# A two-layer decoder step on one core: weights split further ahead, products ordered by kind, memory caches loaded earlier, norm sums on GpSimd

## The chip, the cores and the metric

One core of a Trainium2 chip. The metric is the device time of one execution in microseconds (us). The engines are TensorE (PE in the profile), VectorE (DVE), ScalarE (ACT), GpSimd (POOL) and the queue of SyncE (SP), which only issues transfers here. ACT and POOL issue transfers too.

## What is computed

The reference is one inference step of a decoder with two layers over 576 tokens (512 of a prompt, 64 of eight samples), width 1024, all in float32. Each layer has three branches on the same input, which are merged by sigmoid gates and projected; then a squared-ReLU MLP. Cut to what matters:

```
rq, rk, rv, rg, sq, sk, sv, mq, g_r, g_s, g_m = split(x @ w_in)
mk, mv  = mem_prompt @ w_mem_kv              # the prompt's memory; the samples' is cached
ret_b   = (silu(rg) * group_norm(retention(rq, rk, rv))) @ w_br_ret
swa_b   = sliding_window_attention(sq, sk, sv) @ w_br_swa
mem_b   = softmax(mq @ km.T) @ vm @ w_br_mem # km, vm: mk, mv or cache_mem_k, cache_mem_v
merged  = sigmoid(g_r)*ret_b + sigmoid(g_s)*swa_b + sigmoid(g_m)*mem_b
x = layer_norm(ALPHA*x + merged @ w_out)
h = square(relu(x @ w_up))
x = layer_norm(ALPHA*x + h @ w_down)
```

## The kernel before

**Products.** A float32 product is made of three products of rounded parts: with w = hi + lo and x = xh + xl, it sums hi·xh, lo·xh and hi·xl. The tokens stand in two groups, A and B, of 288 columns. A unit is 128 output rows of one weight (a tile of 128x1024, 512 KB): 8 slots of 128 input channels, 3 matmuls each, 24 matmuls for one group. `gemm` writes the three matmuls of a slot after each other.

**Splitting.** A unit of weights is loaded by SP into a T tile (there are 38 of them) and split before use: its hi part is a CAST on ACT or DVE, its lo part a TENSOR_TENSOR on DVE. If its use is more than FAR = 11 us ahead, the lo part is instead a negated copy on ACT and a transfer from POOL that adds the raw weights to it (the T<-T transfers). The order of all instructions is decided while the program is built: `tick` goes through the units in order of use and splits the next one either when ScalarE is expected to be free, or, whatever ScalarE has to do, when its use is less than LEAD = 4 us ahead. A unit that is not split by then is split right ahead of its matmuls (`run`). A cap limits the tiles in flight; it differs by stage.

**Stages of a layer.** Memory keys and values mk, mv; four rounds of retention projections (rk, rq, rv, rg); sliding-window projections; gates and branch outputs (gr, br, gs, bs, gm, bm), between whose matmuls the attention work of the three branches is interleaved by generators; the output projection wo (8 units for A, then 8 for B) with the first norm; the up projection (8 units for A, then 8 for B, and so on); the pairs, which multiply sums and differences of blocks; the down projection dn with the second norm. Then the next layer starts with mk, mv.

**Memory attention of the samples** (`mem_sample`, once for each group and layer) takes four batch entries. Each needs a 512 KB tile of cached keys (in_mck) and later one of cached values (in_mcv), loaded by POOL. Two key tiles are asked for well ahead (`mem_ahead`), the other two after the matmuls of the first and the second:

```
yield Pe((kt[b], qz))
for h in range(4): T.matmul(ps[...], lhsT=qz[:, b, h, :], rhs=kt[b][:, h, :], ...)
if b < 2: kt.append(self.mem_load("mck", l, f * 4 + b + 2))
```

and the value tiles likewise: two after the last key matmul, the others after the first and second value product.

**Norm** (`norm_ev`). Each output unit of wo and dn is added to the residual tile on DVE (T<-T,pg), then to a running sum (accA, accB), and from unit 4 on its square (ACT) to a sum of squares (tiles s, rc). `half` shifts and squares units 0 to 3. After unit 7, `last` takes both sums through PE, forms the reciprocal root on ACT (Ln, Exp) and DVE, subtracts the mean and multiplies on DVE, and makes the xh parts (ACT, 128x288 with par) and xl parts (DVE, 128x576) of the next stage's input. All sums are on DVE.

Every instruction is recorded by one helper, so that the profile shows line L359 nearly everywhere; tiles tell the stages apart. The functions that the change touches follow.

Of the kernel before, what the change touches and what calls it, by code (L numbers as in the profile page):

```python
# [24 lines left out]
EPS = 1e-5  # L25
# [12 lines left out]
EARLY_PE = -0.8  # L38
LEAD = 4.0
FAR = 11.0  # L40
# [409 lines left out]
class Builder:  # L450
# [72 lines left out]
    def soonest(self, choices, *ins):  # L523
# [3 lines left out]
        return getattr(self.nc, min(choices, key=lambda x: max(c.te[x[0]], t) + x[1])[0])  # L527

    def rounded(self, hi, src):
        n = src.free_size()  # L530
        e = self.soonest((("scalar", 0.094 + n / 1200.0), ("vector", 0.2 + n / 1920.0)), src)
        (e.copy if e is self.nc.scalar else e.tensor_copy)(hi, src)
# [14 lines left out]
    def split(self, i):  # L547
        u, k, b = self.items[i]
        if b is not None:
            self.w[i] = self.block(u, b)  # L550
            self.live[i] = 1
            return
        raw = self.raw.pop(u)
        hi = self.tile([P, 8, P], F32R)
        lo = self.tile([P, 8, P], F32R)
        if self.use[i] - self.fill.t > FAR and k[1] not in ("mq", "gs", "bs", "gm", "bm") and u > 15:
            self.nc.scalar.copy(hi, raw)
            self.nc.scalar.activation(lo, raw, AF.Copy, scale=-1.0)
# [65 lines left out]

    def gemm(self, ps, u, slots, xs, first=True):
        hi, lo = self.w[u]
        mm = self.nc.tensor.matmul
        n = len(slots)
        cols = ps.shape[1]
        for i, s in enumerate(slots):  # L630
            xh, xl = xs(i)
            mm(ps, lhsT=hi[:, s, :], rhs=xh, start=(first and i == 0), stop=False, skip_group_check=not first)
            mm(ps, lhsT=lo[:, s, :], rhs=xh, start=False, stop=False, skip_group_check=not first)
            mm(ps, lhsT=hi[:, s, :], rhs=xl, start=False, stop=(i == n - 1), skip_group_check=not first)
            if i % 2 and i < n - 1:
                self.fill.advance(6 * mm_us(cols))

    def mstep(self, u, g, X, evac, slots=range(8), tag="g"):
        n = NG[g]

        def fn():
            ps = self.bank(tag)[:, :n]
            self.gemm(ps, u, list(slots), lambda i: (X[g]["h"][i // 4][:, i % 4, :], X[g]["l"][i // 4][:, i % 4, :]))
            evac(g, ps)
        return ([u], fn, 6 * mm_us(n))

    def both(self, u, X, evac, slots=range(8), tags="gg"):
        return [self.mstep(u, g, X, evac, slots, tag) for g, tag in zip("AB", tags)]

# [180 lines left out]

    def norm_ev(self, g, y, l, gi, eps, out, scale=None):

# [23 lines left out]
        def shift():  # L856
            pm = self.bank("a")[:, :n]
            yield from mean(pm, st["acc"])
            yield (pm,)
            st["c"] = self.u(n)  # L860
            V.tensor_scalar(st["c"], pm, 4.0, None, ALU.mult)
            cb = st["c"].unsqueeze(1).to_broadcast([P, 4, n])
            self.nc.vector.tensor_tensor(y[1], y[1], cb, ALU.subtract)

        def half():
            c = st.pop("c")
            V.tensor_tensor(y[0], y[0], c.unsqueeze(1).to_broadcast([P, 4, n]), ALU.subtract)
            sq = self.tile([P, 4, n])
            S.activation(sq, y[0], AF.Square)
            yield (sq,)  # L870
            V.scalar_tensor_tensor(st["acc"], c, -4.0, st["acc"], ALU.mult, ALU.add)
            self.nc.vector.tensor_tensor(sq[:, 0:2], sq[:, 0:2], sq[:, 2:4], ALU.add)
            self.nc.vector.tensor_tensor(sq[:, 0], sq[:, 0], sq[:, 1], ALU.add)
            self.nc.vector.tensor_tensor(st["s2"], st["s2"], sq[:, 0], ALU.add)

        def last():
# [17 lines left out]
            if out is None:  # L894
                V.tensor_tensor(y[1], y[1], mb, ALU.subtract)
            V.tensor_tensor(y[0], y[0], mb, ALU.subtract)
# [22 lines left out]
            def end(i):  # L919
# [3 lines left out]
                h = out[g]["h"][j][:, k]  # L923
                self.nc.vector.tensor_tensor(out[g]["l"][j][:, k], y[j][:, k], h.bitcast(F32), ALU.subtract)
            if out is not None:
# [28 lines left out]
        def ev(m, ps):  # L954
# [7 lines left out]
            if m == 0:  # L962
# [4 lines left out]
                return  # L967
            self.nc.vector.tensor_tensor(st["acc"], st["acc"], yt, ALU.add)
            if m == 1:
# [7 lines left out]
            elif m > 4:  # L977
# [4 lines left out]
                if m == 7:  # L982
                    self.fill.flush()
                    self.nc.vector.tensor_tensor(st["s2"], st["s2"], sq, ALU.add)
                    st["last"] = last()
                    self.fill.add(st["last"], 0)
                else:
                    self.fill.later(lambda: self.nc.vector.tensor_tensor(st["s2"], st["s2"], sq, ALU.add),
                                    2.0, sq)
# [420 lines left out]
    def mem_sample(self, kt, l, f, mq, ME):  # L1410
# [20 lines left out]
        m = self.small(1, "zm")  # L1431
# [39 lines left out]
    def layer(self, l, X):  # L1471
# [78 lines left out]
        for p in range(4):  # L1550
# [14 lines left out]
            steps += self.both(uid["rk", p], X, rope_ev(1)) + self.both(uid["rq", p], X, rope_ev(0))  # L1565
            if p == 0 and l:
# [238 lines left out]
        for m, g in [(m, g) for g in "AB" for m in range(SKEW_UP)] \  # L1805
                + [(m, g) for m in range(SKEW_UP, 8) for g in "AB"]:
            steps.append(self.lazy(self.mstep(uid["up", m], g, X1, up_ev(m, H[m // 4])), lambda g=g: n1[g].st["last"]))
        self.run(steps, SKEW_UP)
# [55 lines left out]
        if True:  # L1864
            keys = [("dn", m) for m in range(8)]
            n2 = {g: self.norm_ev(g, y[g], l, 16, EPS, X2) for g in "AB"}
            if X2 is not None:
# [90 lines left out]
```

## Time and profile before

| | |
|---|---|
| median of 3 runs | 2208.03 us (2206.8 to 2208.1) |
| profiled execution | 2205.09 us |
| its span (first to last instruction) | 2203.2 us |
| PE busy | 2131.3 us, 97% |
| DVE busy | 1285.2 us, 58% |
| ACT busy | 929.2 us, 42% |
| POOL busy | 151.0 us, 7% |
| mean granted clock of TensorE | 0.983 |

The profile covers one execution. Busy time of PE includes matmuls at a reduced clock: the profile gives the clock that was granted as a share of full speed (1.00 is 2.4 GHz, 0.50 is 1.2 GHz). Times in rows are counted from the start of the span.

### The profile page before, as it was taken

To read this page: it belongs to the slowest core of one execution; us is meant where nothing else is said; L and a number is where in the kernel's file an instruction comes from. 1 tells how busy PE (TensorE), PEld (TensorE's weight loads), DVE (VectorE), ACT (ScalarE), POOL (GpSimd) and SP (SyncE) were. 2 spreads that over 40 slices of the span, in tenths; PEclk is the share of its full clock that TensorE was granted. 3 is DMA by queue.
4 is the path that set the end of the run, shared out by engine and by line. 5 is a ranking of instruction groups with operands and counts; after the bars stand their busy time and mean duration, and the time that the engine had idled before them with its cause. 6 is when DMAs were issued, how large, how long until landed. Compare 5 with 4: busy or idle time off the path is not lost.

```text
span 2203.2 us, 39044 instructions
## 1 busy us (share of the span) xinstructions
PE 2131.3 (97%) x16180; PEld 2066.1 (94%) x16180; DVE 1285.2 (58%) x2752; ACT 929.2 (42%) x1757; POOL 151.0 (7%) x213
## 2 busy tenths in 40 slices
PE   9999999999998999999899999999999989999997
PEld 8999999988998999999889999999899989999997
DVE  6555644454558466666755556444545585666667
ACT  4343355223146445445444333552231465444452
POOL 0111101000000000000011111010000000000000
PEclk9999999999999999999999999999999999999999
DMA  8455745333363422224565556453342634222231
GB/s 310 112 150 138 175 116 122 118 115 133 108 187 87 108 93 96 77 89 153 142 195 141 147 143 173 107 133 106 118 142 96 189 85 116 103 77 87 96 102 57
DMA packets 83297, 277.73 MB, mean 126 GB/s; under 512 B 9072, under 2 KB 18800, under 8 KB 83056
## 3 DMA queue, kind: packets, MB, share of 16 engines
q1 hardware_dynamic: 50944, 168.27, 21.9%
q0 software_dynamic: 27088, 99.10, 19.9%
q10 hardware_dynamic: 5088, 7.87, 1.1%
q8 instruction: 127, 2.08, 0.4%
q14 instruction: 50, 0.41, 0.1%
HBM read 200.89 MB, written 15.99 MB: 98 GB/s over the span
## 4 chain that ended last, share of the span: by engine, by line
PE 85%; issue 6%; DVE 5%; DMA 2%; ACT 1%; SPq 0%; POOL 0%; DVEq 0%; POOLq 0%; ACTq 0%
PE pg L359 63%; PE pa L359 22%; DVE T L359 4%; DMA T<-in_wall 1%; ACT T L359 1%; DMA T<-in_mck 1%; ACT u L359 1%; DMA T<-in_mcv 0%; DMA T<-T 0%; DVE u L359 0%; DVE ln L359 0%; SPq L359 0%; DVE accB L359 0%; DVE rc L359 0%; DVE s L359 0%
## 5 line engine op out<-in xcount | busy, mean ns | idle before, releaser
L359 PE MATMUL pg<-T,T 128*128 128x288 f32 (+1 forms) x11840 | 1648.9, 297 | 33.0 <-DVE T L359 21.6
L359 PEld LDWEIGHTS pg<-T,T 128*128 128x128 f32 x11840 | 1599.5, 190 | 56.9 <-DVE T L359 25.6
L359 PE MATMUL pa<-T,T 128*128 128x288 f32 (+8 forms) x3368 | 456.8, 308 | 20.9 <-DMA T<-in_mck 7.9
L359 ACT CAST T<-T 128x1024 fp32r<-128x1024 f32 (+7 forms) x501 | 383.1, 797 | 185.2 <-DVE T L359 100.7
L359 PEld LDWEIGHTS pa<-T,T 128*128 128x128 f32 (+3 forms) x3368 | 400.0, 176 | 47.2 <-DMA T<-in_mck 10.7
L359 DVE TENSOR_TENSOR T<-T,T 128x1024 fp32r<-128x1024 f32 (+7 forms) x448 | 389.8, 889 | 85.7 <-ACT T L359 75.0
L359 POOL DMA_DIRECT2D T<-T x115 | 98.7, 858 | 1485.1 <-ACT T L359 1092.1
L359 ACT ACTIVATE t<-pg 128x288 f32<-128x288 f32 x128 | 52.7, 412 | 263.8 <-PE pg L359 261.1
L359 ACT ACTIVATE T<-T 128x1024 fp32r<-128x1024 f32 (+1 forms) x127 | 135.5, 1067 | 14.9 <-DVE T L359 10.8
L359 ACT ACTIVATE u<-u 128x288 f32<-128x288 f32 x200 | 88.8, 444 | 92.4 <-DVE u L359 88.4
L359 DVE TENSOR_TENSOR T<-u,T 128x288 fp32r<-128x288 f32 x160 | 72.3, 454 | 77.6 <-ACT T L359 77.6
L359 ACT COPY T<-pg 128x512 f32<-128x512 f32 (+2 forms) x44 | 21.0, 480 | 216.0 <-PE pg L359 216.0
L359 ACT CAST T<-u 128x288 fp32r<-128x288 f32 x160 | 69.3, 433 | 56.3 <-DVE u L359 52.3
L359 DVE TENSOR_TENSOR T<-T,u 128x288 f32<-128x288 f32 (+2 forms) x136 | 88.0, 660 | 3.6
L359 DVE SCALAR_TENSOR_TENSOR T<-t,pg 128x288 f32<-128x288 f32 x64 | 29.0, 453 | 94.0 <-ACT t L359 76.1
L359 DVE TENSOR_TENSOR T<-T,pg 128x288 f32<-128x288 f32 x128 | 57.5, 449 | 38.4 <-PE pg L359 38.0
L359 DVE TENSOR_TENSOR u<-u,pa 128x288 f32<-128x288 f32 x72 | 32.7, 454 | 80.2 <-PE pa L359 79.8
L359 DVE TENSOR_TENSOR T<-pa,T 128x512 fp32r<-128x512 f32 (+2 forms) x48 | 25.1, 534 | 81.0 <-ACT T L359 80.6
L359 DVE TENSOR_TENSOR T<-T,pa 128x288 f32<-128x288 f32 (+1 forms) x92 | 52.2, 568 | 17.7 <-PE pa L359 15.5
L359 DVE SCALAR_TENSOR_TENSOR u<-t,pg 128x288 f32<-128x288 f32 x64 | 28.7, 448 | 44.4 <-PE pg L359 44.4
L359 ACT CAST T<-pa 128x512 fp32r<-128x512 f32 (+2 forms) x40 | 17.3, 438 | 52.9 <-PE pa L359 48.9
L359 PE MATMUL pa<-cst,T 128*128 128x128 f32 (+1 forms) x306 | 39.6, 272 | 0.0
(157 smaller groups left out, 1041.5 us busy)
## 6 DMA issues: line engine op xcount, KB each, us to landing
T<-in_wall SPq DMA_DIRECT2D x305, 512.0 KB, 3.6
T<-T POOLq DMA_DIRECT2D x115, 512.0 KB, 5.5
T<-in_mck POOLq DMA_DIRECT2D x16, 512.0 KB, 4.4
T<-in_mcv POOLq DMA_DIRECT2D x16, 512.0 KB, 5.1
T<-in_s POOLq DMA_DIRECT2D x8, 512.0 KB, 7.6
out_state_s<-T POOLq DMA_DIRECT2D x8, 512.0 KB, 4.0
T<-in_xT SPq DMA_DIRECT2D x4, 576.0 KB, 11.0
T<-in_xT ACTq DMA_DIRECT2D x4, 576.0 KB, 6.8
```

The costliest lines, as they stand in the source:

```text
L359: r = f(*a, **kw)
```

## The change

Six edits. LEAD goes from 4 to 13. `gemm` goes through the slots three times, once for each kind of part; for late="w" the order is hi·xh, hi·xl, lo·xh, for late="x" (the first unit of the retention keys and of up) hi·xh, lo·xh, hi·xl. The two remaining key tiles are asked for right after the masked queries, ahead of the first matmul, and a value tile after each key matmul. The sums of the norms go to DVE or GpSimd, whichever the build's clock expects to be done first (`pick`); in the last norm of a group GpSimd also subtracts the mean from one half and makes one of four multiplications. Of the blocks of dh only the first may be split by way of POOL's transfers. In the down projection of layer 0 the cap is 9 instead of 7, so that the splits of the next layer's memory input may be placed there.

```diff
-LEAD = 4.0
+LEAD = 13.0
...
+    def pick(self, *ins, bias=0.0):
+        n = ins[0].free_size()
+        return self.soonest((("vector", 0.068 + n / 960.0 + bias), ("gpsimd", 0.15 + n / 480.0)), *ins)
...
-        if self.use[i] - self.fill.t > FAR and k[1] not in ("mq", "gs", "bs", "gm", "bm") and u > 15:
+        if self.use[i] - self.fill.t > FAR and k[1] not in ("mq", "gs", "bs", "gm", "bm") and u > 15 \
+                and (k[1] != "dh" or k[2] == 0):
...
-        for i, s in enumerate(slots):
-            xh, xl = xs(i)
-            mm(ps, lhsT=hi[:, s, :], rhs=xh, start=(first and i == 0), stop=False, skip_group_check=not first)
-            mm(ps, lhsT=lo[:, s, :], rhs=xh, start=False, stop=False, skip_group_check=not first)
-            mm(ps, lhsT=hi[:, s, :], rhs=xl, start=False, stop=(i == n - 1), skip_group_check=not first)
-            if i % 2 and i < n - 1:
-                self.fill.advance(6 * mm_us(cols))
+        order = ((hi, 0), (hi, 1), (lo, 0)) if late == "w" else ((hi, 0), (lo, 0), (hi, 1))
+        for k, (w, e) in enumerate(order):
+            for i, s in enumerate(slots):
+                j = k * n + i
+                self.nc.tensor.matmul(ps, lhsT=w[:, s, :], rhs=xs(i)[e], start=(first and j == 0), stop=(j == 3 * n - 1),
+                                      skip_group_check=not first)
+                if j % 6 == 5 and j < 3 * n - 1:
+                    self.fill.advance(6 * mm_us(cols))
...
             if out is None:
-                V.tensor_tensor(y[1], y[1], mb, ALU.subtract)
+                G.tensor_tensor(y[1], y[1], mb, ALU.subtract)
...
-                V.tensor_tensor(y[j][:, k], y[j][:, k], rb, ALU.mult)
+                e = G if i == 3 and out is None else V
+                e.tensor_tensor(y[j][:, k], y[j][:, k], rb, ALU.mult)
...
-            self.nc.vector.tensor_tensor(st["acc"], st["acc"], yt, ALU.add)
+            self.pick(yt, st["acc"], bias=0.0 if m in (1, 7) else bias).tensor_tensor(st["acc"], st["acc"], yt, ALU.add)
...
+        kt += [self.mem_load("mck", l, f * 4 + b) for b in (2, 3)]
+        vt = []
...
-            if b < 2:
-                kt.append(self.mem_load("mck", l, f * 4 + b + 2))
-        vt = [self.mem_load("mcv", l, f * 4 + b) for b in range(2)]
+            vt.append(self.mem_load("mcv", l, f * 4 + b))
...
-            if b < 2:
-                vt.append(self.mem_load("mcv", l, f * 4 + b + 2))
...
-                     7 if X2 else 8)
+                     9 if X2 else 8)
```

In the built program POOL issues 21 more T<-T transfers and gets 58 additions and multiplications (most of 128x288) and one ISA instruction ahead of the first of them; DVE has 79 fewer TENSOR_TENSOR and 20 more CAST, ACT 20 fewer CAST and 21 more ACTIVATE. The number of matmuls and of SP's transfers is the same. Three places follow; numbers behind an underscore are tile numbers in the order in which the program asks for them, and "-" is a row of before, "+" one of the change.

POOL, memory attention of group A in layer 0, the key and value tiles behind the two that are asked for ahead:

```order
 L359 DMA T_5010<-in_mck 128x1024
 L359 DMA T_5012<-in_mck 128x1024
-L359 DMA T_5336<-in_mck 128x1024
-L359 DMA T_5342<-in_mck 128x1024
+L359 DMA T_5270<-in_mck 128x1024
+L359 DMA T_5272<-in_mck 128x1024
+L359 DMA T_5340<-in_mcv 128x1024
+L359 DMA T_5346<-in_mcv 128x1024
 L359 DMA T_5352<-in_mcv 128x1024
-L359 DMA T_5354<-in_mcv 128x1024
-L359 DMA T_5456<-in_mcv 128x1024
-L359 DMA T_5466<-in_mcv 128x1024
```

The key tiles were the 5336th and 5342nd tile asked for and are the 5270th and 5272nd; the last two value tiles were asked for about a hundred tiles after the first two, and now stand in one run with them.

ACT, end of the branch outputs and start of the output projection in layer 0. T_6653 (before) and T_6632 (now) are the raw weights of wo's unit 1 (the second), T_6734 now those of unit 2, t and u belong to the branch outputs. Before:

```order
L359 ACTIVATE t_6732<-pg_6707 128x288
L359 CAST T_5891<-u_6747 128x288
L359 CAST T_5895<-u_6765 128x288
L359 CAST T_5891<-u_6783 128x288
L359 CAST T_5895<-u_6801 128x288
L1778 ACT_TABLE_LOAD
L359 CAST T_6822<-T_6653 128x1024
```

Now:

```order
L359 ACTIVATE t_6732<-pg_6707 128x288
L359 CAST T_6736<-T_6632 128x1024
L359 ACTIVATE T_6737<-T_6632 128x1024
L359 CAST T_5891<-u_6754 128x288
L359 CAST T_5895<-u_6772 128x288
L359 CAST T_5891<-u_6790 128x288
L359 CAST T_5895<-u_6808 128x288
L1784 ACT_TABLE_LOAD
L359 CAST T_6829<-T_6734 128x1024
```

The second unit of the output projection was cast behind the table load, and is now cast and copied ahead of four branch outputs, its lo part by way of POOL.

ACT, the norm of group B in layer 0 (ln tiles) between the evacuations of up's units for group A (pg to u to T). Before:

```order
L359 ACTIVATE ln_7588<-pa_7428 128x288
L359 ACTIVATE ln_7599<-u_7596 128x288
L359 ACTIVATE ln_7599<-ln_7599 128x288
L359 ACTIVATE u_7616<-pg_7579 128x288
L359 ACTIVATE u_7616<-u_7616 128x288
L359 CAST T_7434<-u_7616 128x288
L359 CAST T_7648<-T_7521 128x1024
```

Now:

```order
L359 ACTIVATE ln_7618<-pa_7430 128x288
L359 ACTIVATE u_7626<-pg_7597 128x288
L359 ACTIVATE u_7626<-u_7626 128x288
L359 CAST T_7436<-u_7626 128x288
L359 ACTIVATE u_7656<-pg_7631 128x288
L359 ACTIVATE u_7656<-u_7656 128x288
L359 CAST T_7436<-u_7656 128x288
L359 ACTIVATE ln_7663<-u_7660 128x288
L359 ACTIVATE ln_7663<-ln_7663 128x288
```

Ln and Exp of the norm stood right behind its square, and now stand behind the evacuations of two of group A's units; the cast of the weights that followed is no longer at this place.

## Rows read from the trace of the kernel before

**Rows 1.** The page, busy time of each engine.
```profile
PE 2131.3 (97%) x16180; PEld 2066.1 (94%) x16180; DVE 1285.2 (58%) x2752; ACT 929.2 (42%) x1757; POOL 151.0 (7%) x213
```

**Rows 2.** What PE waited for: total us, times, longest us.
```profile
PE pg L359 <- DVE T L359: 21.6, 15, 4.1
...
PE pg L359 <- ACT T L359: 11.1, 4, 7.5
...
PE pa L359 <- DMA T<-in_mck: 7.9, 4, 3.8
...
PE pa L359 <- DMA T<-in_mcv: 7.9, 4, 3.8
```

**Rows 3.** Timeline, memory attention, layer 0: start us, us, engine, work, [idle before].
```profile
481.25 1.05 POOL L359 DMA_DIRECT2D T<-in_mck  x2 [30.37 <-PE pa L359]
...
485.18 1.08 PE L359 MATMUL pa<-T,T 128*32 128x256 f32 x8 [3.82 <-DMA T<-in_mck]
...
498.02 0.53 POOL L359 DMA_DIRECT2D T<-in_mcv  x1 [0.43 <-PE pa L359]
...
501.97 1.08 PE L359 MATMUL pa<-T,T 128*32 128x128 f32 x16 [3.83 <-DMA T<-in_mcv]
```

**Rows 4.** Stretches at half clock, both layers: us, PE busy, PEclk, DMA share, GB/s.
```profile
483.30:490.13 6.83, 4.76 (x27) 0.50 0.82 314
...
500.37:507.19 6.82, 5.05 (x44) 0.50 0.43 154
...
1582.39:1589.22 6.83, 5.75 (x31) 0.50 0.83 315
...
1599.46:1606.28 6.82, 5.73 (x47) 0.50 0.38 133
```

**Rows 5.** The page, DMA issues: KB each, median us from issue to landing.
```profile
T<-T POOLq DMA_DIRECT2D x115, 512.0 KB, 5.5
...
T<-in_mck POOLq DMA_DIRECT2D x16, 512.0 KB, 4.4
```

**Rows 6.** Timeline of PE, second output-projection unit, layer 0.
```profile
631.46 0.40 PE L359 MATMUL pg<-T,T 128*128 128x288 f32 x1 [1.38 <-ACT T L359]
...
632.72 1.68 PE L359 MATMUL pg<-T,T 128*128 128x288 f32 x8 [0.86 <-DVE T L359]
```

**Rows 7.** Stretches at half clock: output projection, up projection, start of layer 1.
```profile
633.49:636.90 3.41, 3.41 (x17) 0.50 0.46 157
...
705.17:711.99 6.82, 5.00 (x21) 0.50 0.20 77
...
1090.87:1101.11 10.24, 4.01 (x17) 0.50 0.27 91
```

**Rows 8.** Timeline, up projection of layer 0, from group A to group B.
```profile
706.99 5.68 PE L359 MATMUL pg<-T,T 128*128 128x288 f32 x24 [3.77 <-DVE T L359]
...
714.76 9.50 PE L359 MATMUL pg<-T,T 128*128 128x288 f32 x58 [2.09 <-DVE T L359]
...
722.83 0.41 ACT L359 ACTIVATE u<-pg 128x288 f32<-128x288 f32 x1 [1.84 <-PE pg L359]
```

**Rows 9.** Timeline of PE, memory keys and values, start of layer 1.
```profile
1096.33 0.80 PE L359 MATMUL pg<-T,T 128*128 128x256 f32 x2 [7.48 <-ACT T L359]
...
1117.75 7.34 PE L359 MATMUL pg<-T,T 128*128 128x512 f32 x24 [3.44 <-DVE T L359]
```

**Rows 10.** Timeline of PE, start of the down projection, layer 0.
```profile
1026.47 0.40 PE L359 MATMUL pa<-T,T 128*128 128x288 f32 x1 [1.01 <-ACT T L359]
...
1036.50 5.73 PE L359 MATMUL pg<-T,T 128*128 128x288 f32 x41 [0.86 <-DVE T L359]
```

**Rows 11.** Timeline of DVE, last norm of the program.
```profile
2191.27 2.62 DVE L359 TENSOR_TENSOR T<-T,u 128x1152 f32<-128x1152 f32 x2
```

**Rows 12.** Groups by form: busy us, mean ns of one, idle before.
```profile
L359 ACT CAST T<-T 128x1024 fp32r<-128x1024 f32 x231 | 239.6, 1046 | 40.6 <-PE pg L359 23.8 <-DMA T<-in_wall 7.2 <-issue 6.3
...
L359 DVE TENSOR_TENSOR accB<-accB,T 128x288 f32<-128x288 f32 x28 | 12.8, 458 | 1.0
```

More of the change, by code (lines that the diff above doesn't have):

```diff
@@ L623, in run, with gemm, mstep @@
                 self.fill.advance(tick)
-    def gemm(self, ps, u, slots, xs, first=True):
+    def gemm(self, ps, u, slots, xs, first=True, late="w"):
         hi, lo = self.w[u]
-        mm = self.nc.tensor.matmul
         n = len(slots)
         cols = ps.shape[1]
-        for i, s in enumerate(slots):
-            xh, xl = xs(i)
-            mm(ps, lhsT=hi[:, s, :], rhs=xh, start=(first and i == 0), stop=False, skip_group_check=not first)
-            mm(ps, lhsT=lo[:, s, :], rhs=xh, start=False, stop=False, skip_group_check=not first)
-            mm(ps, lhsT=hi[:, s, :], rhs=xl, start=False, stop=(i == n - 1), skip_group_check=not first)
-            if i % 2 and i < n - 1:
-                self.fill.advance(6 * mm_us(cols))
-    def mstep(self, u, g, X, evac, slots=range(8), tag="g"):
+        order = ((hi, 0), (hi, 1), (lo, 0)) if late == "w" else ((hi, 0), (lo, 0), (hi, 1))
[6 more added lines that the diff above has]
+                    self.fill.advance(6 * mm_us(cols))
+    def mstep(self, u, g, X, evac, slots=range(8), tag="g", late="w"):
         n = NG[g]
@@ L642, in fn, with both @@
             ps = self.bank(tag)[:, :n]
-            self.gemm(ps, u, list(slots), lambda i: (X[g]["h"][i // 4][:, i % 4, :], X[g]["l"][i // 4][:, i % 4, :]))
+            self.gemm(ps, u, list(slots), lambda i: (X[g]["h"][i // 4][:, i % 4, :], X[g]["l"][i // 4][:, i % 4, :]),
+                      late=late)
             evac(g, ps)
         return ([u], fn, 6 * mm_us(n))
-    def both(self, u, X, evac, slots=range(8), tags="gg"):
-        return [self.mstep(u, g, X, evac, slots, tag) for g, tag in zip("AB", tags)]
+    def both(self, u, X, evac, slots=range(8), tags="gg", late="w"):
+        return [self.mstep(u, g, X, evac, slots, tag, late) for g, tag in zip("AB", tags)]
     def pair_steps(self, key, XT, evac):
@@ L829, in rsqrt, with norm_ev @@
             V.scalar_tensor_tensor(out, a, 1.5, out, ALU.add, ALU.mult)
-    def norm_ev(self, g, y, l, gi, eps, out, scale=None):
+    def norm_ev(self, g, y, l, gi, eps, out, scale=None, bias=1.0):
         nc = self.nc
@@ L862, in shift @@
             cb = st["c"].unsqueeze(1).to_broadcast([P, 4, n])
-            self.nc.vector.tensor_tensor(y[1], y[1], cb, ALU.subtract)
+            self.pick(y[1], st["c"], bias=bias).tensor_tensor(y[1], y[1], cb, ALU.subtract)
         def half():
@@ L871, in half @@
             V.scalar_tensor_tensor(st["acc"], c, -4.0, st["acc"], ALU.mult, ALU.add)
-            self.nc.vector.tensor_tensor(sq[:, 0:2], sq[:, 0:2], sq[:, 2:4], ALU.add)
-            self.nc.vector.tensor_tensor(sq[:, 0], sq[:, 0], sq[:, 1], ALU.add)
-            self.nc.vector.tensor_tensor(st["s2"], st["s2"], sq[:, 0], ALU.add)
+            self.pick(sq[:, 0:2], sq[:, 2:4], bias=bias).tensor_tensor(sq[:, 0:2], sq[:, 0:2], sq[:, 2:4], ALU.add)
+            self.pick(sq[:, 0], sq[:, 1], bias=bias).tensor_tensor(sq[:, 0], sq[:, 0], sq[:, 1], ALU.add)
+            self.pick(st["s2"], sq[:, 0], bias=bias).tensor_tensor(st["s2"], st["s2"], sq[:, 0], ALU.add)
         def last():
@@ L923, in end @@
                 h = out[g]["h"][j][:, k]
-                self.nc.vector.tensor_tensor(out[g]["l"][j][:, k], y[j][:, k], h.bitcast(F32), ALU.subtract)
+                self.pick(y[j][:, k], h).tensor_tensor(out[g]["l"][j][:, k], y[j][:, k], h.bitcast(F32), ALU.subtract)
             if out is not None:
@@ L983, in ev @@
                     self.fill.flush()
-                    self.nc.vector.tensor_tensor(st["s2"], st["s2"], sq, ALU.add)
+                    self.pick(sq, st["s2"]).tensor_tensor(st["s2"], st["s2"], sq, ALU.add)
                     st["last"] = last()
@@ L987, in ev @@
                 else:
-                    self.fill.later(lambda: self.nc.vector.tensor_tensor(st["s2"], st["s2"], sq, ALU.add),
+                    self.fill.later(lambda: self.pick(sq, st["s2"], bias=bias).tensor_tensor(st["s2"], st["s2"], sq, ALU.add),
                                     2.0, sq)
@@ L1564, in rope_ev @@
                 return ev
-            steps += self.both(uid["rk", p], X, rope_ev(1)) + self.both(uid["rq", p], X, rope_ev(0))
+            steps += self.both(uid["rk", p], X, rope_ev(1), late="w" if p else "x") + self.both(uid["rq", p], X, rope_ev(0))
             if p == 0 and l:
@@ L1806, in layer @@
                 + [(m, g) for m in range(SKEW_UP, 8) for g in "AB"]:
-            steps.append(self.lazy(self.mstep(uid["up", m], g, X1, up_ev(m, H[m // 4])), lambda g=g: n1[g].st["last"]))
+            steps.append(self.lazy(self.mstep(uid["up", m], g, X1, up_ev(m, H[m // 4]), late="x" if m == 0 else "w"), lambda g=g: n1[g].st["last"]))
         self.run(steps, SKEW_UP)
@@ L1865, in layer @@
             keys = [("dn", m) for m in range(8)]
-            n2 = {g: self.norm_ev(g, y[g], l, 16, EPS, X2) for g in "AB"}
+            n2 = {g: self.norm_ev(g, y[g], l, 16, EPS, X2, bias=0.0 if g == "A" and X2 is None else 1.0) for g in "AB"}
             if X2 is not None:
```

## The prediction

> **What bounds the kernel.** The page first: PE is busy for 2131.3 of 2203.2 us, every other engine for at most 58% [rows 1]. So a gain can come from two places alone: the 72 us in which PE stands still, and the stretches in which it works at half clock. The list of PE's waits [rows 2] says what it stands for: 15.8 us for cached keys and values of the memory (four waits each, the longest 3.8), 21.6 us for tiles from DVE and 11.1 us for tiles from ACT. The reader should see that these are few and long. The timeline then places them, and the windows show their second price: at each of the longer ones the granted clock falls from 1.00 to 0.50, the lower of its two levels (1.2 of 2.4 GHz), and stays there for 3.4 to 10.2 us [rows 4, 7]. A matmul in such a stretch takes twice its time, so half of PE's busy time in it is lost.
>
> **The change, place by place.** Times are taken from the profiled execution (2205.09 us) and the difference is then laid on the median, 2208.03 us.
>
> *Memory caches.* Before, the third key tile is issued at 481.25 by POOL, since it waits for the tile that PE's first key product frees, and PE stands for 3.82 us until it lands; the third value tile is issued at 498.02 and PE stands for 3.83 us [rows 3]. Over both layers that is 15.8 us [rows 2], and four stretches at half clock with 4.76 + 5.05 + 5.75 + 5.73 = 21.3 us of PE's work [rows 4], of which half is lost: 10.65. Together 26.4 us. The change asks for all tiles earlier. The values are then issued between 482 and 492 and are wanted only after 497: with 4.4 us from issue to landing [rows 5] for a key tile, which has the size of a value tile, nothing is left of that wait. The keys gain less. An earlier request is no earlier transfer: the tile's slot must be free. By the program, the third key's slot is freed by a DVE multiplication shortly before PE comes to the keys (about 4.7 us before the old issue), the fourth's by a matmul at about 479. So the third lands at about 481, when PE arrives, and the fourth at about 479 + 4.4 = 483.4, while PE wants it at about 481.9. I leave 1.8 us per layer, and one of two stretches at half clock (2.6). Gain 26.4 - 3.6 - 2.6 = **20**. Bounds: 26.4 (nothing left) and 13 (the keys' half untouched). The second group's tiles of each layer are not waited for now, nor later.
>
> *Output projection.* In both layers PE stands for the second unit's split, 1.38 us for hi and 0.86 for lo [rows 6], and then works 3.41 us at half clock [rows 7]: 1.38 + 0.86 + 1.7 = 3.9. With the change this unit is cast ahead of four branch outputs, about 10 us earlier; its lo part lands 5.5 us after POOL issues it [rows 5], and is wanted only for the last 8 of 24 matmuls. Nothing remains. Gain **7.9**; lower bound 5, if the next unit's cast, now behind the table load, is late.
>
> *Up projection.* PE stands 3.77 and 2.09 us for lo parts that wait behind the norm of group B in DVE's queue [rows 8], and loses 5.00 / 2 us at half clock after the first of them [rows 7], and some more after the second. The splits now come by ACT and POOL, so group A's eight units end at about 703.2 + 2 x 3.2 = 709.6. But then PE wants group B's norm. Its Ln and Exp stood right behind its square on ACT, and now stand behind two evacuations, and DVE's root steps behind three. Stepping through both queues, 0.46 us for a 288-column row [rows 12], about 0.75 for 576 and 1.3 for 1152 [rows 11], xh is ready from 711 to 715 and xl at 720.2. So the first unit of B ends at about 720.5, where before it ended at 722.8 [rows 8]. The wait takes the place of the old one: 2.3 us less, minus a stretch at half clock (1.5). Gain 0.8 per layer, **1.6**; bounds -4 and +5.
>
> *Start of layer 1.* PE stands 7.48 us, then 3.44 us [rows 9], and loses 4.01 / 2 at half clock [rows 7]: 12.9 us, because the splits of the memory input and of mk and mv are queued behind the norm. With cap 9 the memory input is split during dn, and these waits go. What is late next is again group B's norm: the first product of B in layer 1 must wait for it. By the same stepping this product ends about 5 us earlier than before, and a new dip costs 1. Gain **4**; bounds 0 and 12.9.
>
> *Start of the down projection.* PE's waits here are small, 1.01 and 0.86 us and some of 0.3 [rows 10]. The change loses. LEAD = 13 puts the first dn splits into ACT's and DVE's queues ahead of the last evacuations of the pairs: three casts of 1.05 us [rows 12] and their subtractions stand where the evacuation of the block that PE wants next stood. Stepping through gives waits of 1.4 + 1.8 + 2.7 us in layer 0 (before about 2.4) and 0.5 + 1.6 + 2.8 in layer 1 (before 3.5): 4.9 lost, plus about 1 for clock. Loss **6**; bounds 0 and 11.
>
> *Norm sums on GpSimd.* No row shows an elementwise instruction on POOL. It is bounded from below by DVE's 0.458 us for a 288-column addition [rows 12], at which it would be free or a gain (58 rows off DVE, which is not the bound); from above I take three times that, by which a stage's four or five additions in a row finish 4 us later, 6 us over the kernel where they are at the end of a chain. Most are in the middle of a stage, with units of 3.2 us between them, so I take 0. In the last norm one subtraction of 1.31 us [rows 11] leaves DVE's chain at the end of the program and runs beside it: gain **1.3**, bounds 0 and 2.
>
> The Trainium skill speaks against this edit. "GPSIMD Engine Reference" (2.1 Instruction dispatch, 3.1 Elementwise) gives a two-input elementwise operation there at about twice VectorE's time, and some 6 us more at the first call of newly loaded code; "SBUF — State Buffer" (SBUF: two separate sides) says that a VectorE operation with two SBUF inputs and a GpSimd operation that reads SBUF exclude each other for a whole instruction. No row of this trace shows either; with one delay of 6 us the sum below would be -22.8 instead of -28.8, and a delay at every stage is rival D.
>
> *Order of the three products, dh's blocks.* No matmul is added; late="w" gives lo parts 2 us more, counted above. DVE has time for the dh splits that come back to it (58% busy). 0.
>
> Sum: -20 - 7.9 - 1.6 - 4 + 6 - 1.3 = -28.8. 2208.0 - 28.8 = **2179 us**. PE's idle time should fall from 72 to some 45 us.
>
> **The rivals.** *B. The norms of group B are not in the way.* If their rows on ACT and DVE are done sooner than my stepping says (DVE has 79 fewer subtractions and sums to do), the up projection and layer 1 give back 5 and 9 more, dn costs 3 less: 2208 - 46 = 2162. For it: DVE is idle for 42% of the span. Against: the chain is serial, and the rows that it waits for are ahead of it in the queues.
>
> *C. The caches come no earlier.* If the key slots are freed later than I think, or POOL's queue is held at an earlier request (its transfers wait in order), the keys' half stays: 13 us of 26, and the sum is -16 to -22 + 6: about 2192. For it: only PE's last old reader frees the fourth slot.
>
> *D. Slower: POOL becomes the place that PE waits for.* POOL runs in order, and at the four norm stages its additions stand between the T<-T transfers of the weights. An addition that waits for its input holds the lo part of the next unit, and a lo part is then late by more than the 2 us that the order hi, hi, lo gives. A wait like that of layer 1's start costs 7.48 + 2.0 = 9.5 us [rows 7, 9]; one at each of the four stages gives +38: 2208 - 28.8 + 38 = 2217. It decides from 7.2 us per stage. Against: POOL is busy for 7% [rows 1], and units are split 13 us ahead. The two pages of the Trainium skill that are named above speak for it.
>
> *E. No change*: new waits at dn, up and layer 1 eat what the caches and the output projection give, 28 us at these six places, each near its bad bound.
>
> **How the numbers follow.** The main case has 0.58, B 0.13, C 0.17, D 0.07, E 0.05. 2179 is the main case's; its own range, from the bounds of its terms taken half together, is 2170 to 2189. To leave out no more than 2 in 10 the range must take in most of B and C: 2163 to 2197. A difference of 0.2% (4.4 us) is about what a measurement of this kernel can tell from none. Faster: main, B, C = 0.88; same: E, 0.05; slower: D, 0.07.
>
> **What would show it.** Right: no wait for in_mcv, at most 2 us per layer for in_mck, no half clock around 500; no wait at the output projection's second unit; a wait for the xh or xl of group B (ACT or DVE T tiles) of 6 to 10 us in all at up's and layer 1's ninth and third unit; longer waits than before at dn's start. Wrong: POOL's additions as releasers of PE or of DVE's norm rows for more than 2 us at a stage (D), in_mck waits of nearly 4 us (C), or up's group B starting without a wait (B).

## The result and the profile after

The changed kernel takes 2179.15 us in the median of 4 runs (2171.27 to 2182.62), against 2207.43 us for the kernel before; the ratio is 0.9867, with a 95% interval of 0.984 to 0.9894. That is 28.3 us less.

First the page of the changed kernel: its span and the busy times. The span of this execution is 2169.1 us, 34.1 less than in the trace of before. PE's idle time fell from 72 to 51 us, and its busy time by 13 us, without one matmul less [rows 1]. In a second execution, shown below, the busy time is 2127.3 us, only 4 less than before, and the idle time 52.

```profile
span 2169.1 us, 39184 instructions
...
PE 2118.1 (98%) x16180; PEld 2054.7 (95%) x16180; DVE 1266.0 (58%) x2693; ACT 931.4 (43%) x1758; POOL 236.2 (11%) x292
```

The list of PE's waits answers to [rows 2]: total us, times, longest us. in_mcv is gone, DVE's T tiles are down from 21.6 to 1.3 us, and ACT's T tiles have taken the first place with 15.8.

```profile
PE pg L359 <- ACT T L359: 15.8, 9, 4.6
...
PE pa L359 <- DMA T<-in_mck: 6.4, 2, 3.3
...
PE pa L359 <- DVE u L359: 3.5, 5, 1.2
...
PE pg L359 <- DVE T L359: 1.3, 3, 0.7
```

The stretches at half clock in layer 0 and at the start of layer 1 answer to [rows 4, 7]: after the key tiles, at up, at dn and at the start of layer 1. The one after the value tiles and the one at the output projection are gone. The one at dn is new: the trace of before is at full clock there, in both layers.

```profile
485.35:488.75 3.40, 2.97 (x16) 0.50 0.20 75
...
700.35:707.15 6.80, 6.55 (x21) 0.51 0.00 0
...
1024.50:1027.90 3.40, 3.18 (x13) 0.53 0.96 231
...
1109.95:1120.15 10.20, 6.89 (x20) 0.50 0.85 212
```

**Where the time went.** PE executes 16180 matmuls in both traces. The start of the n-th in one trace less that of the n-th in the other shows how far ahead the changed kernel is; how this grows from stage to stage gives each place its share. The table is worked out in this way from the start times of the traces, for the changed kernel and for the runs described below (in us, minus is faster; layers 0 and 1 as 0 and 1; "end" is from the last matmuls to the end of the span):

```
                start  caches0   wo0   up0   dn0  layer1 caches1  wo1   up1 pairs1   dn1   end   span
after             1.1     -8.3  -4.3  -2.6   3.4    -6.6    -7.6 -4.2  -1.2   -7.0   2.0   1.9  -34.1
again             3.2     -6.8  -4.3  -2.1   3.4    -6.6    -8.7 -4.3  -1.3    0.0   2.1   1.9  -24.3
mem_only         -0.2     -9.8   0.0   0.0   0.0     0.1    -9.5  0.0   1.5    0.0   0.0   0.1  -17.7
order_only       -0.2     -0.1  -2.7  -6.6  -0.9     0.1    -0.7 -2.7  -2.4    0.0   1.4   0.2  -15.0
order_lead13      3.5     -0.1  -4.3  -2.5   3.4     0.1    -0.1 -3.8  -1.5    0.0   2.1   0.0   -3.9
sums_dve          2.7     -8.2  -4.3  -2.0   3.2    -5.2    -7.7 -4.3  -0.9    0.0   2.1   0.0  -25.4
lead4            -0.8     -8.0  -2.7  -8.5  -0.9    -9.1    -9.0 -2.7  -7.0    0.0   1.6   1.9  -45.9
lead4_last        0.7     -8.1  -2.9  -8.5  -1.2    -9.1    -9.0 -2.7  -7.0    0.0   0.1   0.1  -48.4
lead4_cap7       -0.6     -7.1  -2.7  -8.5  -0.9    -8.9    -9.0 -2.6  -7.0    0.0   2.7   1.9  -43.5
lead4_sums_dve   -1.5     -8.1  -2.7  -6.6  -0.9    -4.5    -8.8 -2.6  -2.6    0.0   1.4   0.0  -37.5
up13             -0.9     -7.8  -2.7  -2.0  -0.9    -9.1    -9.0 -2.7  -2.3    0.0   1.6   2.2  -34.3
dn13             -0.8     -7.8  -2.7  -8.5   1.1    -9.8   -10.6 -2.6  -7.0    0.0   2.6   1.9  -45.0
keys3_wo13       -1.0     -9.9  -4.3  -8.5  -0.9    -8.3    -8.9 -4.3  -7.0    0.0   1.6  -0.3  -52.5
```

(Between these places about 0.7 us more are gained in small steps in most rows; the last column is the difference of the spans.) How far one execution can stand from another is seen in lead4 and lead4_last, whose engines get the same instructions in the same order up to the last norm: they differ by 1.5 us at the start and at dn1, and by at most 0.3 at every other place ahead of it. The changed kernel's -34.1 contains 7.0 us in the pairs of layer 1 that belong to this one execution and not to the program, as the second run below shows. Without them it is 27.1 us, near the 28.3 of the medians; in the second run both the spans and the medians differ by 24.3 us.

### The profile page after: what moved, and what is told of

Read it like the earlier page. It is cut to its first block, busy times and chain, and to the rows that moved or that the text cites. A ratio compares the mean times of both kernels' runs of the same rounds, so it can differ in the third digit from the quotient of the medians.

```text
span 2169.1 us, 39184 instructions
## 1 busy us (share of the span) xinstructions
PE 2118.1 (98%) x16180; PEld 2054.7 (95%) x16180; DVE 1266.0 (58%) x2693; ACT 931.4 (43%) x1758; POOL 236.2 (11%) x292
## 4 chain that ended last, share of the span: by engine, by line
PE 91%; DVE 4%; issue 2%; ACT 2%; DMA 2%; POOL 0%; SPq 0%; DVEq 0%; POOLq 0%; ACTq 0%
PE pg L359 68%; PE pa L359 22%; DVE T L359 3%; ACT T L359 1%; DMA T<-in_wall 1%; ACT u L359 1%; DVE u L359 1%; DMA T<-in_mck 1%; DMA T<-T 0%; DVE ln L359 0%; DVE accA L359 0%; DVE s L359 0%; POOL T L359 0%; ACT t L359 0%; SPq L359 0%
## 5 line engine op out<-in xcount | busy, mean ns | idle before, releaser
L359 PE MATMUL pg<-T,T 128*128 128x288 f32 (+1 forms) x11840 | 1644.1, 297 | 20.4 <-ACT T L359 15.8
L359 ACT CAST T<-T 128x1024 fp32r<-128x1024 f32 (+7 forms) x483 | 368.7, 788 | 224.0 <-DVE T L359 174.3
L359 PE MATMUL pa<-T,T 128*128 128x288 f32 (+8 forms) x3368 | 447.7, 303 | 10.4 <-DMA T<-in_mck 6.4
L359 DVE TENSOR_TENSOR T<-T,T 128x512 fp32r<-128x512 f32 (+8 forms) x427 | 370.9, 880 | 92.2 <-ACT T L359 82.8
L359 POOL DMA_DIRECT2D T<-T x136 | 118.7, 883 | 1375.4 <-ACT T L359 963.0
L359 ACT ACTIVATE T<-T 128x1024 fp32r<-128x1024 f32 (+1 forms) x148 | 157.5, 1065 | 10.5 <-DVE T L359 8.2
L359 DVE CAST T<-T 128x1024 fp32r<-128x1024 f32 (+1 forms) x52 | 35.8, 689 | 6.8 <-PE pa L359 4.8
```

What stands on the lines that cost most here:

```text
L359: r = f(*a, **kw)
```

## The experiments

The ratios are to the kernel before, on the same chip; all runs have 4 to 7 timings. The theory was that each edit acts at its own place: caches, order of products and early splits give, and splitting ahead loses a little at dn. The rivals were that the gain comes from one edit alone, or from VectorE having less to do.

**again: the changed kernel once more, no edit.**

> The changed kernel once more, unaltered. In its profile shown above the pairs of layer 1 run 300 matmuls in 39.0 us, those of layer 0 in 40.0, as before had it in both layers: 7 us that no step of the change accounts for. If that belongs to the order of the program, this profile shows 39.0 again and the time is near 2171 us. If it belongs to the execution, the profile shows 40.0 in both layers and about 2178 us, and the runs spread over some 10 us.

Measured: 2181.05 us (2173.16 to 2182.19), ratio 0.988 (0.9865 to 0.9896). The windows show the pairs of layer 0 and of layer 1, first for the trace shown above, then for this one: length, PE busy with the number of matmuls, granted clock, DMA share, GB/s.

```profile
740.00:1000.00 260.00, 260.00 (x1953) 1.00 0.28 89
...
1800.00:2050.00 250.00, 250.00 (x1926) 1.00 0.31 95
```

```profile
740.00:1000.00 260.00, 260.00 (x1952) 1.00 0.27 89
...
1800.00:2050.00 250.00, 250.00 (x1877) 1.00 0.31 95
```

PE is busy throughout at full granted clock in all four. A matmul takes 260 / 1953 = 133.1 ns in layer 0 and 250 / 1926 = 129.8 ns in layer 1 of the first trace, and 133.2 in both layers of the second. So the 7 us belong to the execution; the two fastest of the nine runs of this kernel, 2171 and 2173 us, would fit with it, but only one of them has a trace.

**mem_only: the earlier requests for keys and values, alone.** Before, with:

```diff
+        kt += [self.mem_load("mck", l, f * 4 + b) for b in (2, 3)]
+        vt = []
...
-            if b < 2:
-                kt.append(self.mem_load("mck", l, f * 4 + b + 2))
-        vt = [self.mem_load("mcv", l, f * 4 + b) for b in range(2)]
+            vt.append(self.mem_load("mcv", l, f * 4 + b))
...
-            if b < 2:
-                vt.append(self.mem_load("mcv", l, f * 4 + b + 2))
```

> Before with the earlier requests for memory keys and values alone. If the parts of the change act each at its own place, as the difference of the two traces reads (8.3 us in layer 0, 7.8 in layer 1), this takes 16 us: about 2191 us. A wait of about 3 us stays at the last key tile in each layer, none at the values. Rival, the earlier transfers only collide with the weights' (then the gain is half or less): 2199 us or more.

Measured: 2188.01 us, ratio 0.9919 (0.9905 to 0.9932), 17.3 us less in the medians; 9.8 and 9.5 us at the two places, nothing elsewhere but 1.5 lost at up1. The theory holds. What stays is the last key tile. The timeline of the changed kernel shows why it takes PE 3.3 us, where [rows 3] showed 3.82 for the third tile:

```profile
477.62 0.53 POOL L359 DMA_DIRECT2D T<-in_mck  x1 [26.02 <-DVE T L359]
...
479.99 0.53 POOL L359 DMA_DIRECT2D T<-in_mck  x1 [1.84 <-PE pg L359]
...
480.25 0.33 SPq L359 DMA_DIRECT2D T<-in_wall  x1
...
485.78 1.08 PE L359 MATMUL pa<-T,T 128*32 128x256 f32 x8 [3.32 <-DMA T<-in_mck]
```

The fourth key tile is issued at 479.99, released by PE as the prediction read from the program, and 0.3 us later SP issues a unit of weights. The key tile then needs 5.7 us to land instead of the median 4.4 of [rows 5]; the 16 key tiles of this trace take 3.8 to 5.7 us. That the two transfers slow each other is a reading of these times; no run separates them.

**order_only: the order of the three products, alone.** Before, with the change's `gemm` and its `late` arguments.

> Before with the order of the three kinds of products alone (hi xh, hi xl, lo xh for a whole unit). Theory: the waits for lo parts go, 8.5 and 7.0 us at up as in the run with LEAD = 4, and 2 us in each layer at the output projection, while keys, values and the start of layer 1 stay as before: 19 to 20 us, about 2186 us. Rival, the lo parts at up come in time because they are split by way of POOL, not because they are wanted later: then up keeps most of its 10 us and this is at 2200 us or more.

Measured: 2190.46 us, ratio 0.9926 (0.9913 to 0.9939), 15.1 us less in the medians. The order is what removes most of up's loss in layer 0 (6.6 us) and 2.7 us in each layer at the output projection; at up in layer 1 it gave 2.4 where 7.0 were expected. The rival is out for layer 0; for layer 1 something else is missing (see lead4_sums_dve).

**order_lead13: the same with LEAD = 13.**

```diff
-LEAD = 4.0
+LEAD = 13.0
```

> The run before this one with LEAD = 13, nothing else. Theory: splitting ahead whatever ScalarE has to do costs time by itself: the rows of the norm of group B wait behind splits and evacuations in ACT's queue (up 6 us in layer 0, 5 in layer 1), and dn starts 4 us later in layer 0; the output projection gives back 2 us in each layer. 10 to 18 us slower than with the order alone. Rival, the loss belongs to the sums that went to GpSimd or to cap 9: then this is within 3 us of it.

Measured: 2198.67 us, ratio 0.9968 (0.9958 to 0.9978). That is 8.2 us slower than the order alone, somewhat less than the 10 to 18 expected: start +3.7, up0 +4.1, dn0 +4.3, output projection -1.6 and -1.1. The sums are on VectorE and the cap is 7 here, so the loss belongs to LEAD. LEAD = 13 with the products in the old order was not tried.

**lead4: the change with LEAD = 4.**

> The changed kernel with LEAD = 4 as before. Theory: the wait at the output projection's second unit comes back for its hi part (1.4 us and a stretch at half clock, 3 us in each layer) and up loses some, 4 us in both, while the start of the down projection gets its 5.4 us back: 2178 to 2186 us. Rival, splitting ahead is where most of the gain besides the caches comes from, and the rest hangs on it: 2190 us or more.

Measured: 2159.0 us (2156.84 to 2160.24), ratio 0.9787 (0.9773 to 0.98): 20 us faster than the change with LEAD = 13, where 1 us faster to 7 us slower was expected. Both my theory and its rival fall. By the table LEAD = 13 costs 2 to 4 us at the start, 6 at each up, 4.3 at dn0, 2.5 at layer 1, and gives 1.6 us at each output projection. How it costs 6 us at up0 is seen in the timelines of ACT, DVE and PE. With LEAD = 13 (the changed kernel):

```profile
692.48 0.44 ACT L359 ACTIVATE ln<-u 128x288 f32<-128x288 f32 x1
...
692.95 0.45 ACT L359 ACTIVATE ln<-ln 128x288 f32<-128x288 f32 x1
...
696.18 0.45 DVE L359 TENSOR_TENSOR ln<-ln 128x288 f32<-128x288 f32 x1
...
698.87 4.48 ACT L359 ACTIVATE T<-T,par 128x288 fp32r<-128x288 f32 x8
...
699.55 7.82 PE L359 MATMUL pg<-T,T 128*128 128x288 f32 x22 [1.97 <-ACT T L359]
```

With LEAD = 4:

```profile
686.99 0.45 ACT L359 ACTIVATE ln<-u 128x288 f32<-128x288 f32 x1 [0.58 <-DVE u L359]
...
687.47 0.44 ACT L359 ACTIVATE ln<-ln 128x288 f32<-128x288 f32 x1
...
688.13 0.45 DVE L359 TENSOR_TENSOR ln<-ln 128x288 f32<-128x288 f32 x1
...
692.60 2.18 ACT L359 ACTIVATE T<-T,par 128x288 fp32r<-128x288 f32 x4
...
701.96 10.26 PE L359 MATMUL pg<-T,T 128*128 128x288 f32 x75 [0.94 <-DVE T L359]
```

The reader should see the two ln rows of ACT (Ln, Exp) and the affine rows (T<-T,par) that make xh. At LEAD = 4 Ln is done at 687.4, and the first xh rows stand at 692.60, while PE is still in group A; PE's only wait in this stretch is 0.94 us, and the granted clock is 1.00 throughout. At LEAD = 13 PE gets through group A without a wait, but Ln starts at 692.48, DVE's root at 696.18 and xh at 698.87; PE starts group B at 699.55 with a wait of 1.97 us and then follows the affine rows one by one, 22 matmuls in 7.82 us, at half clock from 700.35 to 707.15.

**up13: the change with LEAD = 13 for up's units alone.**

```diff
-        urgent = self.use[i] < self.fill.t + LEAD
+        urgent = self.use[i] < self.fill.t + (13.0 if self.items[i][1][1] == "up" else LEAD)
```

> The change with LEAD = 13 for the units of up alone and 4 for all others. Theory: LEAD = 13 costs its time place by place; at up the Ln and Exp of group B's norm stand behind evacuations of group A again, PE waits for the first unit of B, and up gives 2 to 4 us in layer 0 and 1 to 2 in layer 1 instead of 8.5 and 7.0; the rest is as with LEAD = 4: 2169 to 2171 us. Rival, the 20 us are an effect of the whole program (transfers of all units, tiles held longer): less than 4 us of them come from here.

Measured: 2171.86 us, ratio 0.9841 (0.9828 to 0.9855), 12.9 us slower than LEAD = 4 everywhere. The two ups give 2.0 and 2.3 us instead of 8.5 and 7.0; no other place moves by more than 0.3. Here the cause of the larger part of the 20 us is shown: early splits of up's own units.

**dn13: the same for dn's units alone.**

> The change with LEAD = 13 for the units of the down projection alone. Theory, by the difference of the traces at LEAD = 13 and 4: the start of the down projection of layer 0 is 4.3 us later, of layer 1 0.5, and the start of layer 1 2.7: 2165 to 2167 us. Rival, these waits come from the splits of the units ahead of it: 2159 to 2161 us.

Measured: 2163.08 us (2160.03 to 2164.78), ratio 0.98 (0.9787 to 0.9814), some 4 us slower than LEAD = 4, but the runs and the intervals of the two overlap. The traces show 2.0 us at dn0, a place that differs by no more than 0.3 among the seven other traces with the new order of products and LEAD = 4 there. The 1.0 at dn1 is less than lead4 and lead4_last differ by. So nearly half of dn0's 4.3 us comes from splits of dn itself; where the rest comes from is open. The prediction of it missed by 2 to 4 us.

**sums_dve: the change with all norm work on VectorE.**

```diff
-        return self.soonest((("vector", 0.068 + n / 960.0 + bias), ("gpsimd", 0.15 + n / 480.0)), *ins)
+        return self.nc.vector
...
-                G.tensor_tensor(y[1], y[1], mb, ALU.subtract)
+                V.tensor_tensor(y[1], y[1], mb, ALU.subtract)
...
-                e = G if i == 3 and out is None else V
+                e = V
```

> The changed kernel with every sum of the norms, and the subtraction and multiplication of the last norm, on VectorE again. Theory: GpSimd's sums give nothing, and at the last norm VectorE stands while GpSimd works (3.73 us for a row of 1.31), so this is 2 us faster or equal: 2175 to 2179 us, with the last norm's subtraction at 1.31 us again. Rival, the norms of group B are shorter because their sums left VectorE: then this is 4 us or more slower (2183 us or more), with longer waits of PE at the start of group B in up and in layer 1.

Measured: 2178.39 us (2176.41 to 2179.63), ratio 0.9875 (0.9861 to 0.9888), as the change itself within its spread. At the end it gains 1.9 us, at layer 1 it loses 1.4. With LEAD = 13, GpSimd's 58 rows together are worth nothing that the medians show.

**lead4_sums_dve: the same with LEAD = 4.**

> The change with LEAD = 4 and all norm work on VectorE. Against the run with only the last norm back (2156.5 us) it shows what the other 54 rows on GpSimd are worth when ScalarE is not held by splits. Theory from the two up projections (8.5 and 7.0 us with these sums on GpSimd, 6.6 and 2.4 with the order alone): they free VectorE for lo parts there, worth 2 and 4.6 us: 2163 us. Rival, GpSimd's rows give nothing here either: 2157 us or less.

Measured: 2170.11 us, ratio 0.9836 (0.9823 to 0.9849): 13.6 us slower than lead4_last, twice what was expected, and the rival is out. The places are up0 (1.9), up1 (4.4), layer 1 (4.6) and dn1 (1.3), against 2.2 gained at the start; the two traces differ by 10.9 us in all. At up1 the lo part of the seventh unit stands behind rows of the norm (T<-T,u) on DVE, and PE waits for it with that unit's last 8 matmuls for group A:

```profile
1766.73 1.43 DVE L359 TENSOR_TENSOR T<-T,u 128x576 f32<-128x576 f32 x2
...
1768.44 1.22 DVE L359 TENSOR_TENSOR T<-T,T 128x1024 fp32r<-128x1024 f32 x1
...
1769.71 1.57 PE L359 MATMUL pg<-T,T 128*128 128x288 f32 x8 [2.12 <-DVE T L359]
```

With the sums on GpSimd (lead4) this lo part is the second of the two below, done at 1754.05; the matmul that waited above starts at 1761.39 there, and PE goes through group A without a wait:

```profile
1751.69 2.36 DVE L359 TENSOR_TENSOR T<-T,T 128x1024 fp32r<-128x1024 f32 x2 [0.50 <-ACT T L359]
```

So at LEAD = 4 the sums on GpSimd are worth much; at up1 the traces show why, with lo parts that VectorE has ready in time. That they are worth nothing at LEAD = 13 because the norm waits in ACT's queue there is a reading of the timelines above; no run separates it. The sums are also what was missing at up1 in the run with the order alone (2.4 us there, 2.6 here).

**lead4_cap7: LEAD = 4 and the cap of dn back at 7.**

```diff
-                     9 if X2 else 8)
+                     7 if X2 else 8)
```

> The change with LEAD = 4 and the cap of the first down projection back at 7. Theory: cap 9 alone moves the splits of the memory input into the down projection, and they are the 9.4 us at the start of layer 1: 2168 us, with PE's wait of 7.5 us there again. Rival, these splits come early because VectorE lost the norm's sums: then this stays within 3 us of 2159.

Measured: 2158.58 us, ratio 0.9788 (0.9774 to 0.9801): no difference. PE's wait of 7.48 us at the start of layer 1 [rows 9] stays away with cap 7 as with cap 9 (its longest wait for an ACT tile is 2.0 us in both), and the theory falls for LEAD = 4; with LEAD = 13 cap 7 was not tried in the changed kernel. With the sums on VectorE, cap 7 in order_only and order_lead13 gains nothing at layer 1, and cap 9 in lead4_sums_dve and sums_dve gains 4.5 and 5.2 us. These pairs differ in the caches and dh's blocks too; the caches alone give nothing there (mem_only), the rule for dh's blocks was not run alone. So either the sums on GpSimd or cap 9 with that rule seems to be enough for a good part of it.

**lead4_last: LEAD = 4 and the last norm's rows on VectorE.** The second and third edit of sums_dve.

> The change with LEAD = 4 and the last norm's subtraction and multiplication on VectorE. Theory: a row of 1152 columns on GpSimd takes 2.6 us and VectorE stands meanwhile; the end of the program is 1.9 us shorter: 2157 us where LEAD = 4 alone had 2159.0. Rival, the two do work side by side and only my reading of the queues is off: no change or 1 us slower.

Measured: 2156.47 us (2156.22 to 2157.11), ratio 0.9779 (0.9766 to 0.9792), 2.5 us less than lead4; in the traces the end takes 1.8 us less. The timeline of DVE and POOL in the last norm of the changed kernel:

```profile
2155.15 2.62 POOL L359 TENSOR_TENSOR T<-T,u 128x1152 f32<-128x1152 f32 x1 [4.28 <-ACT u L359]
...
2155.24 3.73 DVE L359 TENSOR_TENSOR T<-T,u 128x1152 f32<-128x1152 f32 x1
...
2160.37 3.30 DVE L359 TENSOR_TENSOR T<-T,u 128x576 f32<-128x576 f32 x3
...
2160.48 1.91 POOL L359 TENSOR_TENSOR T<-T,u 128x576 f32<-128x576 f32 x1 [2.71 <-DVE u L359]
```

And of DVE with these rows back:

```profile
2142.88 2.62 DVE L359 TENSOR_TENSOR T<-T,u 128x1152 f32<-128x1152 f32 x2
...
2146.88 2.77 DVE L359 TENSOR_TENSOR T<-T,u 128x576 f32<-128x576 f32 x4
```

Beside a row of 2.62 us on POOL, DVE's row of 1152 columns takes 3.73 us; alone two such rows take 2.62. Of the 3.73 us 2.4 are waiting, and DVE's row ends 1.20 us after POOL's, about its time alone. The same is seen in the multiplications: three rows beside POOL's one take 3.30 us, four alone 2.77.

**keys3_wo13: a version that beats both.** lead4_last, three key tiles asked for ahead instead of two, and LEAD = 13 for the units of the output projection alone.

> The kernel of the run before with two more edits: three of four key tiles are asked for ahead, the fourth before the first key product, and LEAD is 13 for the units of the output projection alone. Theory: the waits of 3.5 and 3.0 us for the last key tile and the half clock behind them go (4 to 5 us in each layer), and 1.4 us with its half clock at the output projection's second unit (2 us in each layer): 2143 to 2147 us. Rival, the key tile that is held longer takes a slot that the weights' splits need: no better than 2157 us.

Measured: 2154.36 us (2152.53 to 2154.9), ratio 0.9767 (0.9755 to 0.978): 2.1 us better than lead4_last, not the 9 to 13 expected. The output projection gives its 1.4 to 1.6 us in each layer. The keys' wait does not go: the fourth tile's request still waits for PE, and PE for the tile. In layer 0 the caches give 1.8 us more all the same: in this trace the granted clock stays at 1.00 after the wait, and lead4_last has a stretch at 0.50 there. In layer 1 they give nothing.

```profile
477.96 0.53 POOL L359 DMA_DIRECT2D T<-in_mck  x1 [27.89 <-PE pg L359]
...
483.58 0.64 PE L359 MATMUL pa<-T,T 128*32 128x256 f32 x8 [3.19 <-DMA T<-in_mck]
```

## Why the prediction was right

The total was right (2179.0 us predicted, 2179.15 measured). The places were right too, save the start and the end of the program; the terms at the places were off by 0.5 to 4.5 us, in both directions, so that much of it cancels. That the total came within 0.2 us is luck: the same kernel once more gave 24.3 us where 28.8 were predicted. PE's idle time was to fall to 45 us and fell to 51.

**Caches**, -20 predicted. The values' waits went as said, and the keys' last wait stayed as said, but 3.3 and 3.1 us long instead of 1.8: 15.5 to 15.9 us in the two traces. The term took the median landing of [rows 5], 4.4 us, for a transfer that took 5.7. This is the wait that C named, at a third of its price.

**Output projection**, -7.9: measured -8.5 and -8.6. But LEAD gives only 1.6 us of it in each layer; the order of the products gives 2.7, since the lo part is no longer wanted by the second matmul.

**Up**, -1.6: measured -3.8 and -3.4, of which 2.6 and 2.1 are in layer 0. The mechanism was right: group A runs through, and PE then waits for group B's norm, behind two evacuations on ACT, and drags along behind the affine rows at half clock. The evacuation of B's first unit in layer 0 starts at 708.32 (row below), where it stood at 722.83 [rows 8]: 14.5 us earlier, of which 11.9 had been gained by then. The gain of 2.6 us was predicted as 2.3. What was mis-sized in layer 0 is the clock: the stretch at half clock, for which 1.5 us were taken off the gain, lies within the time in which PE follows the affine rows and the xl rows anyway, and costs nothing more; the evacuation starts 0.62 us after the last xl row. In layer 1 it does cost: there PE works without a wait at half clock, 24 matmuls in 6.83 us, and the evacuation starts 1.97 us after the last xl row, which puts the cost at some 1.35 us (an estimate, the difference of the two). The gain there is 1.2 and 1.3. The rows are those of layer 0, then of layer 1.

```profile
706.94 0.76 DVE L359 TENSOR_TENSOR T<-T,T 128x576 fp32r<-128x576 f32 x1
...
708.32 0.41 ACT L359 ACTIVATE u<-pg 128x288 f32<-128x288 f32 x1 [4.97 <-PE pg L359]
...
1782.44:1789.27 6.83, 6.83 (x24) 0.50 0.01 2
...
1786.15 0.76 DVE L359 TENSOR_TENSOR T<-T,T 128x576 fp32r<-128x576 f32 x1
...
1788.88 0.41 ACT L359 ACTIVATE u<-pg 128x288 f32<-128x288 f32 x1 [4.54 <-PE pg L359]
```

**Start of layer 1**, -4: measured -6.6, with PE waiting 4.6 us for group B's xh, as said. The step that is not borne out is its cause: "With cap 9 the memory input is split during dn, and these waits go." At LEAD = 4 they go with cap 7 as well (lead4_cap7). How much cap 9 does at LEAD = 13 stays open.

```profile
1112.69 2.16 PE L359 MATMUL pg<-T,T 128*128 128x288 f32 x4 [4.61 <-ACT T L359]
...
1115.42 5.28 PE L359 MATMUL pg<-T,T 128*128 128x288 f32 x18 [0.56 <-ACT T L359]
```

**Start of dn**, +6: measured +5.4 and +5.5, 3.4 of it in layer 0. Against LEAD = 4 that place loses 4.3 us, of which LEAD for dn's own units makes 2.0. The 2.0 and 2.1 in layer 1 belong to LEAD only in part, since order_only and lead4 lose 1.4 and 1.6 there.

**Norm sums on GpSimd**, 0 in the middle: right for this kernel (sums_dve), but not for the reason given, since with LEAD = 4 they are worth 13.6 us.

**Last norm**, -1.3: measured +1.9. The step was "leaves DVE's chain at the end of the program and runs beside it". It doesn't run beside it. The rule of the Trainium skill that stood next to it, "SBUF — State Buffer" (SBUF: two separate sides), says what happened: of a VectorE row with two SBUF inputs and a GpSimd row that reads SBUF, the one that starts first holds the shared port for its whole instruction. The trace agrees, with 3.73 us for a row of 1.31. The Trainium skill, "GPSIMD Engine Reference" (3.1 Elementwise), gives about twice VectorE's time; here the row of 1152 columns took 2.62 to 1.31 us, and the 288-column rows 0.82 to 1.16 in the mean of their groups to 0.458 [rows 12]. The 6 us that the same page of the Trainium skill (2.1 Instruction dispatch) gives for the first call of newly loaded code are not seen in the rows of the first additions: the first took 1.84 us, after 2.51 us of idle time, and the second 0.81.

```profile
636.08 1.84 POOL L359 TENSOR_TENSOR accA<-accA,T 128x288 f32<-128x288 f32 x1 [2.51 <-DVE T L359]
...
639.34 0.81 POOL L359 TENSOR_TENSOR accA<-accA,T 128x288 f32<-128x288 f32 x1 [1.41 <-DVE T L359]
```

**Not foreseen**: the start of the program loses 1.1 to 3.2 us to LEAD = 13, +3.7 in order_lead13 against order_only.

The rival D had the right instruction in the wrong place: POOL holds up DVE, not the weights. And the largest thing that the prediction did not see is a comparison which it never made: the edit that is named first, LEAD, is a loss of 20 us in the company of the others. Its terms were all there, at up "The wait takes the place of the old one", at dn a loss, but each was weighed against before and not against the other edits without it.

## What to carry to other kernels

When several edits are costed together, cost each against the others as well: a term that says "the old wait goes, a new one takes its place" means that two edits compete for the same gain, and the cheaper one alone may keep it whole. Work that is pushed ahead in the queue of an engine is paid for by what stands behind it there, so look for the short serial rows (here Ln and Exp) that the next stage starts from. Let a second vector engine take sums in the middle of a stage, but not half of a row pair at the end of one, where both read SBUF.

## What was not expected of the hardware

A row on VectorE that reads two tiles from SBUF stood for 2.4 of its 3.73 us while a GpSimd row of 1152 columns ran, so that splitting two equal rows over both engines took 1.1 us longer than both on VectorE. And in one execution 1926 matmuls in 250 us ran at 129.8 ns each, where the same program ran at 133.2 ns in another execution and, within the first, at 133.1 ns in the layer before; the granted clock was 1.00 in all. Nothing in the traces shows what sets this.
